# Redrawn side-work tables in a one-layer diffusion step: where weight splits, loads and dot products are emitted, and 69 transferred low parts for 64

## The chip, the cores and the metric

The kernel runs on one core of one Trainium2 chip. The metric is the device time of one execution in microseconds (us); before the change its median is 1312.32 us (three runs, 1312.31 to 1314.57). Lower is better.

## The reference

One inference step of a transformer layer (width 2048, hidden 8192) on two groups of 128 tokens, a prompt ("context") and a sample ("latent"), with the same weights for both:

```python
sh1, sc1, g1, sh2, sc2, g2 = split(silu(c) @ w_ada + b_ada, 6)
h = rms_norm(x) * norm1_w * (1 + sc1) + sh1
qa, ka, va, qb, kb, vb, ga, gb = split(h @ w_in)          # 2048 x 8704
oa = windowed_gqa(rms(qa), rms(ka), va, ...)              # rotary, sink logit, cached context keys
ob = neighbourhood_attention(rms(qb), rms(kb), vb, ...)   # 2-D bias, cached context keys
x = x + g1 * ((sigmoid(ga) * (oa @ w_br_a) + sigmoid(gb) * (ob @ w_br_b)) @ w_out)
h2 = rms_norm(x) * norm2_w * (1 + sc2) + sh2
x = x + g2 * (relu(h2 @ w_up) ** 2 @ w_down)
```

Everything is float32, and the outputs are x of both groups and the prompt's new keys and values.

## The kernel before

**Products in three parts.** TensorE multiplies in a reduced float32 form. Each operand is therefore split into a high part and a low part (the rest), and a product is three: high x high, high x low, low x high. A weight tile is 128 x 1024 (512 KB in `raw`, two row blocks of 512 columns). Its high part `wH` is a rounding copy on ScalarE (`copy`, line 103). Its low part `wL` is made in one of two ways. In the first, VectorE subtracts (`prep_b`, line 265). In the second (`minus_plus`, lines 271 and 272), ScalarE writes the negated high part, and a transfer issued by GpSimd reads the same weights from memory once more and adds them on top. The table `LO_DMA` lists the steps that use the second way, 64 of them.

**Steps.** The program has 456 weight steps in a fixed order, each with one tile and normally 12 matmuls: steps 0 to 71 the first columns of w_in, 72 to 135 the gates, 136 to 167 the branch products, 168 to 199 w_out (the last unit goes through its tiles twice, once for each group), 200 to 215 the first two blocks of w_up, then seven times a pair of up blocks (16 steps, from 216 + 32p) and a down unit (16 steps), and the last down unit from 440. The up pairs use a seven-product scheme over sums of weight blocks: an x step (even) and a y step (odd) together give the tiles `XH`, `XL`, `YB`, `tH`, `tL`, `uH`, `uL`, whose sums are made on VectorE (`y_sums`, `y_split`).

**Order.** Nothing is scheduled by a tool: each engine runs its instructions in the order in which the program emits them, and waits where an operand or a buffer isn't ready. All tiles come from one pool of 54 buffers, so a load waits until a buffer's last reader has finished. The loop `run` goes through the steps. At step i it emits

1. the loads (on SyncE's queue, SP) that stand up to `RUN[i]` steps further on than their place, which is four steps ahead of the step that uses the tile,
2. the transferred low parts of all steps up to i + `LOOK[i]` + 2,
3. the high parts up to i + `LOOK[i]` + `HIA[i]` and the low parts up to i + `LOOK[i]`,
4. the matmuls of step i,
5. the side work that the other tables place at step i.

```python
to = st["i"] + int(LOOK[st["i"]]) + 1
while by_dma and by_dma[0] < to + LO_AHEAD:
    prep_to(by_dma[0] - LO_AHEAD)
    ...
    lo_dma(wsteps[by_dma.pop(0)])
prep_to(to, int(HIA[st["i"]]))
st["mm"](st)
```

**Side work and its tables.** Part of the modulation is made as dot products on VectorE (`dot`, line 1522), two instructions for each entry of `DOTS1`, `DOTS` and `DOTS2`, with a load of 512 KB (`aT`) two steps ahead. The other part goes through TensorE in pairs (`ADA_AT`). `XS_AT` places the scaling of x by its norm. `POST` and `JOBS` place the head norms and the stages of the eight attention jobs. `STAT_AT` places the sums of activations for the up pairs. `M_AT`, `P_UP`, `T_UP` and `U_AT` place the way of an activation block to TensorE's layout: square, two copies into 16-bit planes (`pl`), a transposing transfer on SP (the flip, line 953), a copy that joins the planes (`fTa`), the high part (`a14H` for block 14) and the low part. In `U_AT` the nine numbers of a block are, in this order: relu, square, first plane copy, second plane copy, flip, first join, second join, high part, low part; they count from the first step of the down unit that follows the pair. A down unit that continues a sum starts with a copy of it into the accumulator on ScalarE (`seed`, the rows `acc<-dsum`).

Of the kernel before, what the change touches and what calls it, by code (L numbers as in the profile page):

```python
# [32 lines left out]
FB_DVE = 0  # L33
FB1 = 14
H_AT = 41
DOTS1 = [33, 33, 34, 34, 37, 37, 38, 40]
CHUNKS = [2, 2, 2, 4, 6]
NFAST = 8
FAST = {1: (0, 1, 2, 3, 4, 5, 6, 7), 2: (0, 1, 2, 3, 4, 5, 6, 7), 3: (0, 1, 2, 3, 4, 5, 6, 7), 4: (0, 1, 2, 3, 4, 5, 6, 7), 5: (0, 1, 2, 3, 4, 5, 6, 7), 6: (0, 1, 2, 3, 4, 5, 6, 7), 7: (0, 1, 2, 3, 4, 5, 6, 7)}
# [2 lines left out]
GATE_BACK = 6  # L42
SEED_IN = {3: -1, 4: 0}
SEED_N = (1, 2, 3)
HIA = "743311210111132014324131040001201410000110000000000002332001000011112200212113220010615154541000000011111000021124242135340100000000000031000100414311111003102301703025456797534544530325756887798374954110152262222132244304001211210111020001260102113330004210012121111315222074354363333101001172221556711321013044002233031111121033136010430110000042100334314355141111111100213210101100355521327503258336647833123224414211344122452723573333221344624430000011"
JOIN_LO = 0
SEED_AT = 3
LATE = [1, 0, 0]
ROW_AT = [5, 7, 9, 5]
DIRECT = (3,)  # L50
LO_DMA = [64, 69, 72, 76, 87, 94, 100, 105, 110, 118, 127, 130, 133, 140, 147, 154, 161, 168, 183, 194, 198, 200, 203, 210, 216, 218, 222, 224, 226, 228, 230, 234, 244, 252, 256, 258, 262, 269, 278, 286, 290, 294, 302, 311, 318, 324, 331, 341, 344, 352, 354, 358, 372, 375, 382, 388, 390, 408, 414, 416, 431, 440, 448, 449]
LO_AHEAD = 2

LOOK = "100010111213011164332413300140432203041131331184978600221153115896444435023551503161000543026403132431730112254700160210305438274262151200044577885121102695523366300410132115557812663450155370787570110000735967810745434464433361435371013573632034355244866131031202123201114423542406313307740004014332100388338122762544214363040032331021455957564224713121320243345442298736555517835112330012221110101284023045855132241353731143033251004422430024017145740026"
RUN = "221025555544432133333141100000012151100201121111335457745771402336611111032228530138889867423326226732531445635474877893335887476653143842350364750147441278656355112212111411132451349967889852473322462112246975487815248698865578999999996798443355158999999999987113346242776767998566866777744620011111001121698877377958546288750377448911084554544625666757246225681136864256726310000012522883734579997877872106899999999888999867820057664458624531421113413677"
CONST_AT = [50, 61, 73, 56, 91, 58]
ADA_AT = [None, 5, 11, 23, 23, 41, 28]
XS_AT = {1: 9, 2: 21, 3: 17}
POST = {('kvA', 0): [56, 68, 80], ('qA', 0): [61, 72, 77], ('qA', 1): [72, 73, 79], ('kB', 0): [79, 80, 83], ('qB', 0): [69, 83, 86], ('kB', 1): [92, 95, 101], ('qB', 1): [89, 95, 98]}
JOBS = [[84, 86, 87, 97, 101], [84, 84, 89, 92, 106], [84, 87, 89, 104, 114], [89, 95, 104, 107, 109], [103, 104, 107, 122, 125], [103, 105, 106, 111, 125], [106, 109, 116, 124, 125], [108, 111, 113, 118, 126]]  # L60
SS_AT = [74, 74, 128, 139]
T_AT = [3, 4]
PREP_IN = [5, 7]
DOTS = [45, 56, 56, 56, 56, 56, 56, 56, 57, 57, 60, 62, 63, 64, 65, 68, 72, 72, 72, 75, 78, 79, 79, 82, 83, 84, 84, 86, 88, 90, 90, 92, 93, 94, 96, 98, 98, 98, 99, 103, 105, 105, 107, 107, 109, 109, 111, 113, 113, 113, 114, 117, 121, 121, 122, 122, 123, 123, 126, 127, 131, 131, 132, 133, 133, 134, 134, 138, 139, 140, 141, 142, 144, 145, 146, 152, 153, 157, 158, 159, 160, 162, 166, 169, 174, 175, 178, 178, 179, 180, 183, 186, 187, 189, 190, 190]
DOTS2 = [233, 237, 239, 262, 271, 272, 297, 299, 331, 333, 333, 364, 365, 368, 395, 397, 425, 425, 427, 431, 433, 433, 433, 433, 437, 441, 441, 444, 444, 444, 444, 444]
STAT_AT = [-1, 0, 3, 8]
U_AT = [[[4, 4, 5, 7, 7, 10, 10, 10, 13], [5, 5, 7, 8, 11, 17, 18, 29, 29]], [[1, 1, 4, 4, 4, 5, 10, 26, 26], [10, 11, 11, 13, 13, 19, 27, 27, 27]], [[0, 0, 10, 10, 11, 16, 26, 26, 26], [11, 11, 13, 19, 20, 32, 32, 33, 33]], [[1, 1, 2, 4, 5, 9, 9, 11, 13], [2, 7, 7, 7, 7, 9, 12, 28, 28]], [[7, 9, 9, 9, 13, 19, 25, 25, 30], [2, 2, 2, 2, 5, 10, 12, 12, 16]], [[1, 2, 4, 4, 5, 9, 9, 11, 11], [2, 4, 4, 4, 6, 11, 11, 16, 18]], [[4, 7, 7, 7, 8, 10, 10, 14, 14], [2, 9, 9, 9, 10, 12, 13, 13, 14]]]
XLO_IN = True
STAY = [(3, 1), (3, 2), (5, 2), (5, 3)]
TL_DMA = [2, 3]  # L70
M_TE = (3,)
M_AT = [3, 10, 10]
FLIP = 2
P_UP = [2, 6]
T_UP = [6, 16]
COL = {"qA": 0, "kvA": 1024, "qB": 1536, "kB": 2560, "vB": 3584, "gA": 4608, "gB": 6656}


# [1 line left out]
def tile_hybrid_step(ctx: ExitStack, tc: tile.TileContext, a):  # L80
# [131 lines left out]
    def at(i, fn):  # L212
        cal.setdefault(i, []).append(fn)
# [5 lines left out]
    def load_at(i, fn):  # L219

        loads.append((i, len(loads), fn))
# [68 lines left out]

    by_dma = sorted(LO_DMA)

    def run():
        loads.sort(key=lambda x: x[:2])
        for st in wsteps:
            while loads and loads[0][0] <= st["i"] + int(RUN[st["i"]]):
                loads.pop(0)[2]()
            for j in sorted(j for j in pre if j <= st["i"]):
                for fn in pre.pop(j):
                    fn()  # L300
            to = st["i"] + int(LOOK[st["i"]]) + 1
            while by_dma and by_dma[0] < to + LO_AHEAD:
# [156 lines left out]
    def mod_pair(f):  # L459

        box, k0 = {}, 2 * f
        i = ADA_AT[f]
        for j in range(2):
# [7 lines left out]
    for f in range(1, FB1 // 2):  # L471
        mod_pair(f)
    for g, i in XS_AT.items():
        at(i, lambda g=g: x_scale(g))
# [208 lines left out]
    s0 = len([st for st in wsteps if st["key"] in first_units])  # L683
    load_at(CONST_AT[0], load_consts)
    at(CONST_AT[1], make_consts)
    load_at(CONST_AT[2], load_caches)
    load_at(CONST_AT[3], load_bias)
    for r in range(2):
        at(CONST_AT[4 + r], lambda r=r: mask_bias(r))

# [83 lines left out]

    for u, ps in POST.items():
        nh = 2 if u[0] == "kvA" else 4
# [120 lines left out]
    att_end = 0  # L897
    for (mix, s, g), js in zip([("A", 0, 0), ("A", 1, 0), ("A", 0, 1), ("A", 1, 1), ("B", 0, 0), ("B", 1, 0), ("B", 0, 1), ("B", 1, 1)], JOBS):
        need = [POST["kvA", 0][-1] + 1, POST["qA", g][-1] + 1] if mix == "A" else [
            POST["kB", g][-1] + 1, POST["qB", g][-1] + 1, end_of(("vB", g)) + 1]  # L900
        assert js[0] >= max(need) and list(js) == sorted(js)
# [105 lines left out]
    def br_unit(n):  # L1007
# [195 lines left out]
    def up_unit(n):  # L1203
# [514 lines left out]
```

## Time and profile before

| | |
|---|---|
| median of three runs | 1312.32 us (1312.31 to 1314.57) |
| the profiled execution's own time | 1325.06 us |
| its span, first to last instruction | 1323.3 us |
| mean granted TensorE clock | 0.995 |
| moved by DMA | 430.04 MB |
| transfers of accumulating low parts | 64 of weights, 2 of activations |

In the page's rows a group of instructions reads: line, engine, operation, output tile <- input tiles, shape, count, then busy us, mean ns of one, idle us of the engine just before them and what ended that idle time. In the rows of waits stand the waiting engine, tile and line, what ended the wait, and then total us, times and the longest. In the rows of windows each engine has its busy us; PEclk is the share of TensorE's clock that was granted.

### The profile page before, as it was taken

The numbers are of one execution on the slowest core, as the hardware profiler recorded it, in microseconds if no ns is written. First come the engines' busy times: TensorE is split into PE (matmuls) and PEld (weight loads), VectorE is DVE, ScalarE is ACT, GpSimd is POOL, SyncE is SP. The second block draws the span as 40 slices with busy tenths as digits, with TensorE's granted clock in tenths as the row PEclk, the third lists the DMA queues.
The fourth block names the chain that finished last, engine by engine and source line by source line (L and its number), as shares of the span: only waits on it lengthen the run. The fifth ranks groups of instructions, "written<-read, shape, count | busy, mean of one in ns | idle before, by whom it ended". The sixth has DMA issues, their size and how long they took to land.

```text
span 1323.3 us, 18149 instructions
## 1 busy us (share of the span) xinstructions
PE 1292.9 (98%) x6141; PEld 1047.6 (79%) x6142; DVE 1199.6 (91%) x1584; ACT 963.1 (73%) x1364; POOL 108.1 (8%) x128
## 2 busy tenths in 40 slices
PE   8999999999999999999999999999997999999988
PEld 4787788788888888787878888878886888788876
DVE  4495999999999999999899898999996999999987
ACT  5635668779776665737789897987896878897761
POOL 0000003213000000001101010100000000010110
PEclk9999999999999999999999999999998999999999
DMA  9999999999989999999799999988998999979995
GB/s 373 408 409 401 391 364 328 385 335 326 322 315 376 377 369 338 318 377 311 234 273 279 321 309 342 316 295 294 298 362 152 319 299 276 375 213 377 353 306 184
DMA packets 158285, 430.04 MB, mean 325 GB/s; under 512 B 53056, under 2 KB 54320, under 8 KB 158192
## 3 DMA queue, kind: packets, MB, share of 16 engines
q1 hardware_dynamic: 145264, 383.39, 79.3%
q0 software_dynamic: 12736, 45.39, 16.8%
q8 instruction: 48, 0.79, 0.2%
q14 instruction: 45, 0.37, 0.1%
q10 hardware_dynamic: 192, 0.10, 0.0%
HBM read 402.82 MB, written 14.99 MB: 316 GB/s over the span
## 4 chain that ended last, share of the span: by engine, by line
PE 63%; DMA 11%; issue 11%; DVE 9%; ACT 4%; POOL 1%; DVEq 0%; ACTq 0%; POOLq 0%; SPq 0%
PE acc L324 11%; PE acc L325 11%; PE acc L323 11%; PE acc L434 4%; PE acc L436 4%; PE acc L435 4%; PE Q L1296 4%; PE Q L1295 4%; PE Q L1297 4%; DMA raw<-in_w_down 3%; DMA raw<-in_w_upF 2%; DMA araw<-in_w_pair 1%; PE ps_ada L340 1%; DMA raw<-in_w_in 1%; DVE wL L265 1%
## 5 line engine op out<-in xcount | busy, mean ns | idle before, releaser
L103 ACT ACTIVATE wH<-raw 128x1024 fp32r<-128x1024 f32 (+1 forms) x347 | 347.2, 1043 | 94.6 <-DMA raw<-in_w_down 26.5
L265 DVE TENSOR_TENSOR wL<-raw,wH 128x1024 fp32r<-128x1024 f32 x303 | 356.3, 1222 | 25.0 <-ACT wH L103 14.7
L434 PE MATMUL acc<-wH,hH 128*128 128x512 f32 x276 | 108.5, 393 | 0.0
L436 PE MATMUL acc<-wH,hL 128*128 128x512 f32 x276 | 107.5, 389 | 0.0
L435 PE MATMUL acc<-wL,hH 128*128 128x512 f32 x276 | 107.5, 389 | 0.0
L323 PE MATMUL acc<-wH,hH 128*128 128x512 f32 x256 | 102.8, 402 | 0.0
L324 PE MATMUL acc<-wL,hH 128*128 128x512 f32 x256 | 100.0, 391 | 1.2 <-DVE wL L265 1.2
L325 PE MATMUL acc<-wH,hL 128*128 128x512 f32 x256 | 99.9, 390 | 0.0
L1522 DVE CUSTOM_DVE_ANT_0 junk<-aT,cB,cols 128x1024 uint8<-128x1024 f32 x68 | 87.6, 1288 | 0.8
L1522 DVE CUSTOM_DVE_ANT_0 aT<-aT,cB,cols 128x1024 f32<-128x1024 f32 x68 | 86.2, 1290 | 0.6
L1361 DVE TENSOR_TENSOR t<-raw 128x1024 f32<-128x1024 f32 x56 | 68.2, 1217 | 2.7 <-DMA raw<-in_w_upF 2.3
L1373 DVE TENSOR_TENSOR tL<-t,tH 128x1024 fp32r<-128x1024 f32 x56 | 68.2, 1217 | 2.6 <-ACT tH L103 2.5
L103 ACT ACTIVATE uH<-raw 128x1024 fp32r<-128x1024 f32 x56 | 58.9, 1051 | 13.9 <-DVE raw L1367 10.5
L1373 DVE TENSOR_TENSOR uL<-raw,uH 128x1024 fp32r<-128x1024 f32 x56 | 68.2, 1217 | 0.1
L103 ACT ACTIVATE XH<-raw 128x1024 fp32r<-128x1024 f32 x56 | 58.8, 1050 | 11.2 <-PE Q L1297 4.7
L434 PEld LDWEIGHTS acc<-wH,hH 128*128 128x128 f32 x276 | 51.8, 188 | 12.7 <-issue 2.1
L103 ACT ACTIVATE tH<-t 128x1024 fp32r<-128x1024 f32 x56 | 58.7, 1049 | 2.4 <-DVE t L1361 1.5
L436 PEld LDWEIGHTS acc<-wH,hL 128*128 128x128 f32 x276 | 51.8, 188 | 10.9
L435 PEld LDWEIGHTS acc<-wL,hH 128*128 128x128 f32 x276 | 51.8, 188 | 10.5
L324 PEld LDWEIGHTS acc<-wL,hH 128*128 128x128 f32 x256 | 48.2, 188 | 11.9 <-DVE wL L265 2.1
L325 PEld LDWEIGHTS acc<-wH,hL 128*128 128x128 f32 x256 | 48.1, 188 | 10.2
L323 PEld LDWEIGHTS acc<-wH,hH 128*128 128x128 f32 x256 | 48.1, 188 | 10.0 <-issue 0.5
(668 smaller groups left out, 3465.8 us busy)
## 6 DMA issues: line engine op xcount, KB each, us to landing
raw<-in_w_in SPq DMA_DIRECT2D x133, 512.0 KB, 10.1
raw<-in_w_down SPq DMA_DIRECT2D x128, 512.0 KB, 10.1
raw<-in_w_upF SPq DMA_DIRECT2D x112, 512.0 KB, 6.6
aT<-in_w_adaT SPq DMA_DIRECT2D x72, 512.0 KB, 10.2
aT<-in_w_gT SPq DMA_DIRECT2D x64, 512.0 KB, 10.2
araw<-in_w_pair SPq DMA_DIRECT2D x56, 512.0 KB, 10.1
raw<-in_w_out SPq DMA_DIRECT2D x32, 512.0 KB, 9.6
XL<-in_w_upF POOLq DMA_DIRECT2D x26, 512.0 KB, 8.6
```

The costliest lines, as they stand in the source:

```text
L103: act.activation(out, in_, AF.Copy)
L265: dve.tensor_tensor(st["lo"], st["raw"], st["hi"].bitcast(F32), op=OP.subtract)
L323: pe.matmul(acc[tb], sh, wh[:, k, :], start=f, stop=False, **kw)
L324: pe.matmul(acc[tb], sh, wl[:, k, :], start=False, stop=False, **kw)
L325: pe.matmul(acc[tb], sl, wh[:, k, :], start=False, stop=l, **kw)
L434: pe.matmul(acc[tb], sh, wh[:, k, :], start=kt == 0 and k == 0 and not held and not seeded, stop=False, **kw)
L435: pe.matmul(acc[tb], sh, wl[:, k, :], start=False, stop=False, **kw)
L436: pe.matmul(acc[tb], sl, wh[:, k, :], start=False, stop=last and k == 1 and not hold, **kw)
L1295: pe.matmul(acc, stat[0], hi, start=f, stop=False)
L1361: dve.tensor_tensor(t.rearrange("p (a n) -> p a n", a=2), X.rearrange("p (a n) -> p a n", a=2), Y[:, 0:512].unsqueeze(1).to_broadcast([P, ...
L1373: dve.tensor_tensor(b[n + "L"], v, b[n + "H"].bitcast(F32), op=OP.subtract)
L1522: dve.tensor_tensor_reduce(out, box["raw"], cB[s, tag], 1.0, dst if second else baT[:, part, fb:fb + 1], OP.mult, OP.add, dst)
```

## The change

No function changes, only the tables. Five more steps make their low part by transfer (69), of which 37 are at steps that were not in the list and 32 of the old ones leave it. The tables of loads, look-ahead, dot products, attention jobs, flips and joins all have new values; the number of their entries stays the same. `CONST_AT`, `POST`, `JOBS`, `XS_AT` and the like, not shown, move by some steps in both directions.

```diff
-DOTS1 = [33, 33, 34, 34, 37, 37, 38, 40]
+DOTS1 = [32, 32, 32, 32, 33, 35, 39, 40]
...
-HIA = "743311210111132014324131040001201410000110000000000002332001000011112200212113220010615154541000000011111000021124242135340100000000000031000100414311111003102301703025456797534544530325756887798374954110152262222132244304001211210111020001260102113330004210012121111315222074354363333101001172221556711321013044002233031111121033136010430110000042100334314355141111111100213210101100355521327503258336647833123224414211344122452723573333221344624430000011"
+HIA = "001100001000411222332210054210000242143001000003224543223212012110001000011000245401621101454713440001010010120224222132503400000000013000000000000000010131110211232212338877341224100003402572200201156510010314003222565435425221131010100001070110024131341212000000072722311155142252214431223432124469900111213200011000110121233321000101202101112113334211562210553325232131400121111004000010000000102103626513410000004521221100001322111000002114432895666510"
...
-LO_DMA = [64, 69, 72, 76, 87, 94, 100, 105, 110, 118, 127, 130, 133, 140, 147, 154, 161, 168, 183, 194, 198, 200, 203, 210, 216, 218, 222, 224, 226, 228, 230, 234, 244, 252, 256, 258, 262, 269, 278, 286, 290, 294, 302, 311, 318, 324, 331, 341, 344, 352, 354, 358, 372, 375, 382, 388, 390, 408, 414, 416, 431, 440, 448, 449]
+LO_DMA = [58, 68, 77, 84, 88, 94, 95, 99, 105, 109, 112, 116, 119, 123, 128, 129, 136, 139, 147, 154, 159, 168, 179, 190, 194, 200, 201, 203, 216, 218, 220, 222, 224, 226, 228, 230, 235, 247, 260, 262, 264, 279, 286, 288, 290, 294, 305, 311, 320, 324, 331, 341, 352, 354, 356, 360, 365, 378, 382, 384, 388, 390, 414, 416, 431, 436, 447, 449, 450]
...
-LOOK = "100010111213011164332413300140432203041131331184978600221153115896444435023551503161000543026403132431730112254700160210305438274262151200044577885121102695523366300410132115557812663450155370787570110000735967810745434464433361435371013573632034355244866131031202123201114423542406313307740004014332100388338122762544214363040032331021455957564224713121320243345442298736555517835112330012221110101284023045855132241353731143033251004422430024017145740026"
-RUN = "221025555544432133333141100000012151100201121111335457745771402336611111032228530138889867423326226732531445635474877893335887476653143842350364750147441278656355112212111411132451349967889852473322462112246975487815248698865578999999996798443355158999999999987113346242776767998566866777744620011111001121698877377958546288750377448911084554544625666757246225681136864256726310000012522883734579997877872106899999999888999867820057664458624531421113413677"
...
+LOOK = "042431211022233002010456720126530002442122131444566203233273666985468546244512333161330650346525041211755332033612371521115535201040103365267886563685525772869672131236353222145537254664237378468624325692748837854460100040025676721266676754538440441535778752001112000012016212520524222888985222110220323487888642695697575160520110540363778977011202365562300130020441268427554569010101233034205572624177384155747542741364422354054574858226434305244795322733"
+RUN = "323520002452847511233115361322757443213699552341124866643641212024512326576868461000338955244328413764623367636789889881417522311278788972533554334565450317796251432020000211073450333310002113003787889988857876776180567899998786778888999999897346616379999987997666899899996568798368768999998767879995413303889871498999999999998498788875482311721003768836666702575449999898814586439745458986834777776778888529998777888899998889857113464711476163001122228988"
-ADA_AT = [None, 5, 11, 23, 23, 41, 28]
+ADA_AT = [None, 5, 13, 20, 22, 40, 32]
-XS_AT = {1: 9, 2: 21, 3: 17}
+XS_AT = {1: 11, 2: 11, 3: 8}
...
-STAT_AT = [-1, 0, 3, 8]
-U_AT = [[[4, 4, 5, 7, 7, 10, 10, 10, 13], [5, 5, 7, 8, 11, 17, 18, 29, 29]], [[1, 1, 4, 4, 4, 5, 10, 26, 26], [10, 11, 11, 13, 13, 19, 27, 27, 27]], [[0, 0, 10, 10, 11, 16, 26, 26, 26], [11, 11, 13, 19, 20, 32, 32, 33, 33]], [[1, 1, 2, 4, 5, 9, 9, 11, 13], [2, 7, 7, 7, 7, 9, 12, 28, 28]], [[7, 9, 9, 9, 13, 19, 25, 25, 30], [2, 2, 2, 2, 5, 10, 12, 12, 16]], [[1, 2, 4, 4, 5, 9, 9, 11, 11], [2, 4, 4, 4, 6, 11, 11, 16, 18]], [[4, 7, 7, 7, 8, 10, 10, 14, 14], [2, 9, 9, 9, 10, 12, 13, 13, 14]]]
+STAT_AT = [6, 2, -1, 8]
+U_AT = [[[6, 6, 6, 9, 10, 11, 14, 17, 17], [10, 10, 10, 10, 16, 19, 23, 23, 28]], [[0, 4, 4, 8, 12, 15, 26, 26, 30], [1, 8, 10, 12, 12, 18, 19, 27, 31]], [[3, 7, 9, 9, 10, 21, 26, 28, 29], [6, 13, 19, 19, 21, 27, 28, 31, 32]], [[3, 4, 5, 5, 7, 11, 11, 11, 14], [3, 8, 9, 9, 9, 10, 19, 31, 33]], [[4, 4, 8, 9, 11, 19, 21, 29, 29], [3, 4, 4, 5, 6, 11, 11, 11, 11]], [[0, 2, 4, 5, 5, 8, 8, 14, 14], [1, 9, 9, 10, 10, 24, 25, 28, 28]], [[4, 8, 9, 9, 9, 10, 10, 10, 12], [3, 4, 9, 9, 9, 14, 14, 14, 15]]]
...
-M_AT = [3, 10, 10]
+M_AT = [1, 9, 9]
...
-P_UP = [2, 6]
-T_UP = [6, 16]
+P_UP = [2, 9]
+T_UP = [7, 16]
```

More of the change, by code (lines that the diff above doesn't have):

```diff
@@ L56 @@
-CONST_AT = [50, 61, 73, 56, 91, 58]
-ADA_AT = [None, 5, 11, 23, 23, 41, 28]
-XS_AT = {1: 9, 2: 21, 3: 17}
-POST = {('kvA', 0): [56, 68, 80], ('qA', 0): [61, 72, 77], ('qA', 1): [72, 73, 79], ('kB', 0): [79, 80, 83], ('qB', 0): [69, 83, 86], ('kB', 1): [92, 95, 101], ('qB', 1): [89, 95, 98]}
-JOBS = [[84, 86, 87, 97, 101], [84, 84, 89, 92, 106], [84, 87, 89, 104, 114], [89, 95, 104, 107, 109], [103, 104, 107, 122, 125], [103, 105, 106, 111, 125], [106, 109, 116, 124, 125], [108, 111, 113, 118, 126]]
+LOOK = "042431211022233002010456720126530002442122131444566203233273666985468546244512333161330650346525041211755332033612371521115535201040103365267886563685525772869672131236353222145537254664237378468624325692748837854460100040025676721266676754538440441535778752001112000012016212520524222888985222110220323487888642695697575160520110540363778977011202365562300130020441268427554569010101233034205572624177384155747542741364422354054574858226434305244795322733"
@@ new lines @@
+RUN = "323520002452847511233115361322757443213699552341124866643641212024512326576868461000338955244328413764623367636789889881417522311278788972533554334565450317796251432020000211073450333310002113003787889988857876776180567899998786778888999999897346616379999987997666899899996568798368768999998767879995413303889871498999999999998498788875482311721003768836666702575449999898814586439745458986834777776778888529998777888899998889857113464711476163001122228988"
+CONST_AT = [51, 62, 76, 61, 86, 70]
@@ L61 @@
+ADA_AT = [None, 5, 13, 20, 22, 40, 32]
+XS_AT = {1: 11, 2: 11, 3: 8}
+POST = {('kvA', 0): [60, 71, 76], ('qA', 0): [62, 63, 72], ('qA', 1): [66, 70, 76], ('kB', 0): [73, 74, 87], ('qB', 0): [65, 74, 85], ('kB', 1): [96, 99, 100], ('qB', 1): [87, 100, 104]}
+JOBS = [[81, 82, 89, 99, 102], [78, 82, 89, 96, 110], [82, 83, 91, 107, 110], [87, 99, 103, 106, 109], [99, 104, 107, 113, 125], [102, 102, 106, 114, 127], [109, 109, 116, 119, 121], [107, 111, 112, 116, 125]]
 SS_AT = [74, 74, 128, 139]
@@ L63 @@
 PREP_IN = [5, 7]
-DOTS = [45, 56, 56, 56, 56, 56, 56, 56, 57, 57, 60, 62, 63, 64, 65, 68, 72, 72, 72, 75, 78, 79, 79, 82, 83, 84, 84, 86, 88, 90, 90, 92, 93, 94, 96, 98, 98, 98, 99, 103, 105, 105, 107, 107, 109, 109, 111, 113, 113, 113, 114, 117, 121, 121, 122, 122, 123, 123, 126, 127, 131, 131, 132, 133, 133, 134, 134, 138, 139, 140, 141, 142, 144, 145, 146, 152, 153, 157, 158, 159, 160, 162, 166, 169, 174, 175, 178, 178, 179, 180, 183, 186, 187, 189, 190, 190]
-DOTS2 = [233, 237, 239, 262, 271, 272, 297, 299, 331, 333, 333, 364, 365, 368, 395, 397, 425, 425, 427, 431, 433, 433, 433, 433, 437, 441, 441, 444, 444, 444, 444, 444]
-STAT_AT = [-1, 0, 3, 8]
-U_AT = [[[4, 4, 5, 7, 7, 10, 10, 10, 13], [5, 5, 7, 8, 11, 17, 18, 29, 29]], [[1, 1, 4, 4, 4, 5, 10, 26, 26], [10, 11, 11, 13, 13, 19, 27, 27, 27]], [[0, 0, 10, 10, 11, 16, 26, 26, 26], [11, 11, 13, 19, 20, 32, 32, 33, 33]], [[1, 1, 2, 4, 5, 9, 9, 11, 13], [2, 7, 7, 7, 7, 9, 12, 28, 28]], [[7, 9, 9, 9, 13, 19, 25, 25, 30], [2, 2, 2, 2, 5, 10, 12, 12, 16]], [[1, 2, 4, 4, 5, 9, 9, 11, 11], [2, 4, 4, 4, 6, 11, 11, 16, 18]], [[4, 7, 7, 7, 8, 10, 10, 14, 14], [2, 9, 9, 9, 10, 12, 13, 13, 14]]]
+DOTS = [44, 44, 47, 48, 52, 55, 56, 56, 59, 61, 61, 61, 67, 67, 67, 67, 67, 73, 73, 76, 76, 77, 80, 83, 84, 84, 84, 85, 89, 90, 90, 91, 91, 92, 92, 94, 100, 100, 100, 105, 107, 107, 107, 107, 107, 108, 110, 111, 113, 113, 114, 120, 120, 120, 121, 123, 123, 125, 125, 125, 129, 129, 131, 132, 134, 134, 136, 137, 137, 137, 143, 143, 144, 146, 149, 149, 150, 152, 157, 158, 159, 167, 167, 172, 172, 174, 176, 180, 180, 181, 181, 183, 187, 187, 189, 190]
+DOTS2 = [235, 238, 239, 268, 271, 273, 298, 302, 332, 334, 337, 362, 362, 363, 397, 397, 423, 425, 425, 432, 432, 432, 433, 433, 437, 441, 441, 441, 442, 444, 444, 444]
+STAT_AT = [6, 2, -1, 8]
+U_AT = [[[6, 6, 6, 9, 10, 11, 14, 17, 17], [10, 10, 10, 10, 16, 19, 23, 23, 28]], [[0, 4, 4, 8, 12, 15, 26, 26, 30], [1, 8, 10, 12, 12, 18, 19, 27, 31]], [[3, 7, 9, 9, 10, 21, 26, 28, 29], [6, 13, 19, 19, 21, 27, 28, 31, 32]], [[3, 4, 5, 5, 7, 11, 11, 11, 14], [3, 8, 9, 9, 9, 10, 19, 31, 33]], [[4, 4, 8, 9, 11, 19, 21, 29, 29], [3, 4, 4, 5, 6, 11, 11, 11, 11]], [[0, 2, 4, 5, 5, 8, 8, 14, 14], [1, 9, 9, 10, 10, 24, 25, 28, 28]], [[4, 8, 9, 9, 9, 10, 10, 10, 12], [3, 4, 9, 9, 9, 14, 14, 14, 15]]]
 XLO_IN = True
```

## The prediction

> **What bounds the kernel now.** I read the page first, then who TensorE waited for, then windows around the waits, then single instructions in them.
>
> ```profile
> span 1323.3 us, 18149 instructions
> PE 1292.9 (98%) x6141; PEld 1047.6 (79%) x6142; DVE 1199.6 (91%) x1584; ACT 963.1 (73%) x1364; POOL 108.1 (8%) x128
> ...
> DMA  9999999999989999999799999988998999979995
> ...
> q1 hardware_dynamic: 145264, 383.39, 79.3%
> q0 software_dynamic: 12736, 45.39, 16.8%
> ```
>
> TensorE is busy in 98% of the span: its instructions are the floor, and the change adds and takes none of them. What side work can win is the 30.4 us in which PE is idle (1323.3 - 1292.9) and what a cold clock costs after it. VectorE has 91%, ScalarE 73%, the DMA engines 96% (79.3 + 16.8). The waits of PE, with what ended them (total, times, longest):
>
> ```profile
> PE acc L323 <- ACT acc L103: 5.9, 1, 5.9
> PE acc L323 <- ACT a14H L103: 3.3, 1, 3.3
> PE acc L324 <- DVE wL L265: 2.8, 4, 1.4
> PE acc L1118 <- DVE wL L265: 1.7, 1, 1.7
> ...
> PE Q L1295 <- ACT dsum L103: 1.2, 1, 1.2
> ...
> PE Q L1296 <- DVE tL L1373: 0.8, 1, 0.8
> PE ps_T L930 <- DVE g_gA L1017: 0.7, 1, 0.7
> PE ps_gr L1535 <- DVE gc_g L1522: 0.7, 1, 0.7
> PE acc L325 <- DVE a14L L976: 0.5, 1, 0.5
> ...
> PE Q L1296 <- DMA XL<-in_w_upF: 0.5, 1, 0.5
> ```
>
> Two single waits stand apart from many small ones. In the windows that hold them the clock fell too (PE busy, PEld, DVE, ACT, POOL, PEclk, DMA share, GB/s):
>
> ```profile
> 1000.00:1050.00 50.00, 42.88 (x180) 34.44 (x179) 41.92 (x46) 36.29 (x43) 3.17 (x4) 0.93 0.84 246
> ...
> 1250.00:1300.00 50.00, 46.13 (x196) 37.28 (x195) 45.09 (x62) 32.17 (x39) 5.44 (x8) 0.97 0.95 311
> ```
>
> The first cost 5.9 + 1.2 of wait and 50 x (1 - 0.93) = 3.5 us of clock: 10.6 us. The second cost 3.3 + 0.5 and 50 x (1 - 0.97) = 1.5: 5.3 us. Together 15.9. The profiled execution took 1325.06 us, 1.8 over its span and 12.7 over the median of 1312.32; without these two it would stand at 1309.2. So of the 15.9 us only about 3.1 can be in a timed run, and the small waits (DVE's 2.8 + 1.7 + 0.8 + 0.7 + 0.7 = 6.7) are what the median still has to give. I make the sum against the profile and against the median side by side.
>
> **Part 1: five splits leave VectorE, and the others are put earlier.** A low part made on VectorE is one subtraction (L265). Made by transfer it is a negated copy on ScalarE (L271), an issue on GpSimd (L272) and a second reading of the 512 KB. The rows, busy and mean ns:
>
> ```profile
> L265 DVE TENSOR_TENSOR wL<-raw,wH 128x1024 fp32r<-128x1024 f32 x303 | 356.3, 1222 | 25.0 <-ACT wH L103 14.7
> ...
> L1522 DVE CUSTOM_DVE_ANT_0 junk<-aT,cB,cols 128x1024 uint8<-128x1024 f32 x68 | 87.6, 1288 | 0.8
> ```
>
> ```profile
> L271 ACT ACTIVATE wL<-wH 128x1024 fp32r<-128x1024 f32 x38 | 40.2, 1059 | 1.1 <-PE acc L324 0.2
> ...
> L272 POOL DMA_DIRECT2D XL<-in_w_upF x26 | 22.7, 872 | 221.7 <-ACT XL L271 136.5 <-DVE t L1361 30.4 <-DVE tL L1373 22.1
> ```
>
> VectorE: -5 x 1.222 = -6.1 us. ScalarE: +5 x 1.059 = +5.3 us, covered by its idle 27%; if that cover failed in one place, a copy that PE needs would be 1 us later there. GpSimd: +5 x 0.872 = +4.4 us, covered by its 8%.
>
> Whether 6.1 us of VectorE matter is decided by its queue where PE waits. Step 170 shows it: the split stands behind two dot products, and the DVE runs without a gap.
>
> ```profile
> 140.40 3.49 DVE L265 TENSOR_TENSOR wL<-raw,wH 128x1024 fp32r<-128x1024 f32 x3
> ...
> 549.35 1.28 DVE L1522 CUSTOM_DVE_ANT_0 aT<-aT,cB,shT 128x1024 f32<-128x1024 f32 x1
> ...
> 550.56 3.49 DVE L265 TENSOR_TENSOR wL<-raw,wH 128x1024 fp32r<-128x1024 f32 x3
> ```
>
> ```profile
> 142.02 0.39 PE L434 MATMUL acc<-wH,hH 128*128 128x512 f32 x1
> ...
> 259.15 0.50 PE L324 MATMUL acc<-wL,hH 128*128 128x512 f32 x1 [0.92 <-DVE wL L265]
> ...
> 551.83 0.50 PE L324 MATMUL acc<-wL,m1H 128*128 128x512 f32 x1 [1.39 <-DVE wL L265]
> ```
>
> Following run() with both tables (a split is emitted at the first step i with i + LOOK[i] at or above its own): step 170's is emitted at 169 before (LOOK 3 there) behind 149 splits and 182 dot instructions, and at 167 after (LOOK 6) behind 145 and 178. That is 4 x 1.222 + 4 x 1.288 = 10.0 us less ahead of it, against a wait of 1.39. The same count for the others: step 199 (the 1.7) 175 and 208 become 171 and 207, 6.2 us less; step 101 has 91 and 89, then 90 and 88, 2.5 us less; step 298 has four splits fewer, 4.9 us; step 77 (the 0.92 at 259.15) is itself made by transfer. So all five waits, 2.8 + 1.7 = 4.5 us, should go. Bounds: nothing, if each wait only moves to another split, and -6.7, if all five DVE rows go. I take -4.5, because every one of the five has more taken from ahead of it than it waited. What is late next is the transfers (part 2).
>
> The other VectorE and ScalarE tables (dot products, jobs, x_scale, ADA_AT, STAT_AT) move work between steps and cost no instruction more. They have no price of their own here beyond the queue counts above; one place goes the other way: step 36's split stands behind ten dot instructions of DOTS1 instead of six, 4 x 1.288 = 5.2 us more. It ends at 141.6 (140.40 and a third of 3.49) for a step that PE reaches at 142.02, so the bounds are 0 and +4.8. I take 0, because the loads for these dots are emitted at step 25 instead of 31, so that they need not stand at the same time.
>
> **Part 2: where the transfers now stand.** Of the 69, 14 lie in the gate steps (11 before), and all eight x steps of the first fast pair (216 to 230) have one instead of seven. The nearest row that shows a late one is there: issued at 692.62, it let PE wait at step 224.
>
> ```profile
> 692.62 0.87 POOL L272 DMA_DIRECT2D XL<-in_w_upF  x1 [11.31 <-ACT XL L271]
> ```
>
> ```profile
> 688.69 0.39 PE L1295 MATMUL Q<-XH,h20H 128*128 128x512 f32 x1
> ...
> 703.83 0.50 PE L1296 MATMUL Q<-XL,h22H 128*128 128x512 f32 x1 [0.47 <-DMA XL<-in_w_upF]
> ```
>
> This one took 703.83 - 692.62 = 11.2 us. It was emitted at step 218, which PE began at 688.69, and was of use 15.1 us later. After the change step 224's is emitted at 220 and step 228's at 224, four steps or about 10 us ahead each. Read as time, both would be late by 15.1 - 10 = 5 us: +10. But emission is an order and no time, and ScalarE had 24.77 us of work in these 25:
>
> ```profile
> 687.00:712.00 25.00, 24.53 (x109) 19.94 (x108) 24.71 (x31) 24.77 (x30) 3.46 (x4) 1.00 1.03 243
> 455.00:542.00 87.00, 86.38 (x382) 71.49 (x383) 83.78 (x116) 50.56 (x51) 3.46 (x4) 1.00 1.05 349
> ```
>
> Ahead of these two negations only 1.1 and 1.7 us of its work are added. So the bounds are +1.1 and +10; I take +1.5, as the order is the nearer row. Steps 105 and 112 (three steps ahead, 11 to 12 us) are alike: 0 to +7, taken +0.5.
>
> The five more transfers also load the DMA engines: q0 takes 16.8% x 1323.3 = 222 us for 45.39 MB, so 4.9 us per MB and 2.57 us for 0.524 MB; five make 12.8 us. Bounds 0 (hidden) and +12.8 (every us paid). I take 0: at shares of 1.03 and 1.05 the engines moved 243 GB/s in the one window above and 349 in the other, so the share counts packets that wait as well as bytes, and the loads' queue waits more for buffers than for transfers:
>
> ```profile
> SPq L231 <- PE acc L325: 150.5, 53, 9.3
> ...
> SPq L231 <- DMA raw<-in_w_down: 33.3, 31, 3.2
> ```
>
> The Trainium skill (DMA: Bandwidth & Descriptors, "Issuing engines are not separate DMA queues") speaks against the change here: transfers of all issuers run on the same 16 engines and interleave. By that rule the engines could be the bound, and the sum would be 12.8 us higher; it is weighed as the last rival.
>
> **Part 3: loads earlier, high parts less far ahead.** RUN rises from 4.54 to 5.31 steps in the mean, LOOK from 3.03 to 3.66, HIA falls from 2.10 to 1.76. ScalarE's splits wait for landings:
>
> ```profile
> ACT wH L103 <- DMA raw<-in_w_down: 26.5, 17, 8.5
> ```
>
> More RUN and less HIA mean that ScalarE meets a landed tile more often. The 5.9 us wait is of this kind (a seed copy queued behind a late load). In a timed run I count nothing for it, as little of it recurs there; in the profile 10.6 us. The cost is buffers: the SP row of 150.5 us above says that a load asked for earlier may only wait longer, with SP's flips behind it. Bounds -1.6 and +3; taken 0.
>
> **Part 4: the last pair of relu halves.** a14 was joined at 1258.6 (1255.98 and 2.57), but its copy a14H stood behind the join of a15, which waited for its flip:
>
> ```profile
> 1255.98 2.57 ACT L103 ACTIVATE fTa<-pTa 128x1024 uint16<-128x1024 uint16 x2
> ...
> 1263.46 1.39 ACT L103 ACTIVATE fTa<-pTa 128x1024 uint16<-128x1024 uint16 x1 [4.00 <-DMA pTa<-pla]
> ...
> 1270.94 1.04 ACT L103 ACTIVATE a14H<-fTa 128x1024 fp32r<-128x1024 f32 x1
> ```
>
> U_AT moves that copy from step 438 to 434, ahead of the join of a15. It takes the 5.3 us of this wait away. Against it, both flips are now issued at 433 (432 and 434 before), and a14's join follows one step behind: give back up to 2. Profile: -3.3. Timed: at most 3.1 us of the two disturbances is there, so half of it, -1.5 (bounds -5.3 and +2). M_AT, P_UP and T_UP shift flips and joins by one to three steps and are part of the same bounds.
>
> **The sum.** Median: 1312.3 - 4.5 - 1.5 + 1.5 + 0.5 = 1308.3. Profile: 1325.1 - 4.5 - 10.6 - 3.3 + 2.0 = 1308.7, or 1319 if a late landing like the first recurs.
>
> **Rivals.** (1) The transfers come too late (slower). Steps 224 and 228 pay the 10 us above; with -4.5 and -1.5 that is 1316.3. It decides once the two are more than 4 us late each. For it: 224's has no slack now. Against it: only 1.1 to 1.7 us are put ahead of them. (2) Nothing measurable: for each wait that goes another comes, since PE is busy 98% already and any of 456 steps can be the next late one; 1312. For it: five of the waits here are under 1.4 us, so what frees one step by a few us can cost another as much. (3) More goes than I count: all of DVE's 6.7, the 3.1, the 1.2 and 0.5, with no new wait: 1300.8. (4) The DMA engines are the bound: 12.8 - 6.0 gives 1319.1. For it: share 96%, over 1.00 in the two windows of part 2; against it their GB/s.
>
> **How the numbers follow.** A measurement of this kernel tells 0.2% (2.6 us) from nothing: faster is below 1309.7, slower above 1314.9. Forecast 0.38 (own range 1305 to 1310), rival 3 0.13, rival 2 0.23, rival 1 0.20, rival 4 0.06. A forecast that comes out 1.5 us high falls into "same", one as much low stays faster: I leave 0.50 faster, 0.24 same, 0.26 slower. The range runs from rival 3 to rival 4, 1301 to 1319, and leaves about 0.1 outside.
>
> **What would show it.** Right: L265 x298, L271 x71 in all; no PE wait for wL at L324 or L1118 above 1 us; no wait for a14H; PEclk 1.00 in all windows from 50 us to the end. Wrong: PE waits on XL of 5 us near 703 to 720; the small waits add up to 6 us or more again under other names; the raw loads' time to landing rises by more than 1 us.

## The result, and the profile after

The kernel after takes 1307.81 us (median of 21 runs, 1306.48 to 1314.63) against 1315.05 us for the kernel before beside it (21 runs, 1311.74 to 1321.00): a ratio of 0.9950, with a 95% interval of 0.9936 to 0.9963, so 4.9 to 8.4 us faster. The median of before was 1312.32 in the three runs shown earlier, is 1315.05 here, and lay between 1315.24 and 1317.5 in the sessions of the experiments. Ratios below are therefore always to the runs of before in the same session.

The page of the kernel after, the lines that answer to those of before:

```profile
span 1308.8 us, 18194 instructions
...
PE 1291.1 (99%) x6142; PEld 1045.4 (80%) x6142; DVE 1196.0 (91%) x1579; ACT 964.8 (74%) x1369; POOL 108.9 (8%) x133
...
q1 hardware_dynamic: 145264, 383.39, 79.1%
q0 software_dynamic: 13456, 48.01, 17.6%
...
L265 DVE TENSOR_TENSOR wL<-raw,wH 128x1024 fp32r<-128x1024 f32 x298 | 351.7, 1224 | 26.4 <-ACT wH L103 18.3
```

The profiled execution took 1310.53 us. VectorE has five splits fewer, ScalarE and GpSimd five instructions more, and the accumulating queue moved 2.62 MB more. PE's idle time fell from 30.4 to 17.7 us (1308.8 - 1291.1). The waits of PE in it:

```profile
PE acc L324 <- DVE wL L265: 2.1, 4, 0.8
PE ps_h L1153 <- DVE h2f L1145: 1.5, 1, 1.5
...
PE acc L323 <- ACT wH L103: 1.2, 1, 1.2
...
PE Q L1295 <- ACT up L1187: 0.7, 2, 0.6
PE acc L1228 <- ACT acc L103: 0.7, 1, 0.7
```

The 5.9 us for `acc` and the 3.3 us for `a14H` are gone, and none above 1.5 us has come. The two windows that held them, columns as before:

```profile
1000.00:1050.00 50.00, 50.00 (x222) 41.40 (x221) 48.65 (x55) 43.51 (x50) 3.98 (x5) 1.00 0.89 272
1250.00:1300.00 50.00, 49.28 (x217) 39.77 (x216) 46.99 (x64) 29.05 (x35) 5.91 (x9) 1.00 0.88 292
```

PEclk is 1.00 in both. At the end of the last pair ScalarE now does this:

```profile
1250.44 2.58 ACT L103 ACTIVATE fTa<-pTa 128x1024 uint16<-128x1024 uint16 x2 [3.32 <-PE acc L324]
1253.05 1.06 ACT L103 ACTIVATE a14H<-fTa 128x1024 fp32r<-128x1024 f32 x1
...
1256.02 2.59 ACT L103 ACTIVATE fTa<-pTa 128x1024 uint16<-128x1024 uint16 x2
```

The copy `a14H` stands right behind its own joins and ahead of a15's, and it is done 4.5 us before PE reads it at 1258.6.

### The profile page after: what moved, and what is told of

The parts are those of the page before. It is cut to its first block, busy times and chain, and to the rows that moved or that the text cites. A ratio compares the mean times of both kernels' runs of the same rounds, so it can differ in the third digit from the quotient of the medians.

```text
span 1308.8 us, 18194 instructions
## 1 busy us (share of the span) xinstructions
PE 1291.1 (99%) x6142; PEld 1045.4 (80%) x6142; DVE 1196.0 (91%) x1579; ACT 964.8 (74%) x1369; POOL 108.9 (8%) x133
## 4 chain that ended last, share of the span: by engine, by line
PE 69%; DVE 2%; DMA 2%; ACT 2%; issue 1%; POOL 0%; DVEq 0%; ACTq 0%
PE acc L324 15%; PE acc L325 15%; PE acc L323 15%; PE Q L1296 7%; PE Q L1295 7%; PE Q L1297 7%; DMA pTm<-plm 1%; DMA raw<-in_w_down 1%; DVE wL L265 1%; ACT wH L103 1%; PE ps_PT L858 0%; PE ps_o L882 0%; PE ps_S L811 0%; PE ps_o L886 0%; DVE aT L1522 0%
## 5 line engine op out<-in xcount | busy, mean ns | idle before, releaser
L265 DVE TENSOR_TENSOR wL<-raw,wH 128x1024 fp32r<-128x1024 f32 x298 | 351.7, 1224 | 26.4 <-ACT wH L103 18.3
L103 ACT ACTIVATE uH<-raw 128x1024 fp32r<-128x1024 f32 x56 | 58.8, 1051 | 14.4 <-DVE raw L1367 10.2
L325 PEld LDWEIGHTS acc<-wH,hL 128*128 128x128 f32 x256 | 48.1, 188 | 10.1
## 6 DMA issues: line engine op xcount, KB each, us to landing
raw<-in_w_down SPq DMA_DIRECT2D x128, 512.0 KB, 10.2
aT<-in_w_gT SPq DMA_DIRECT2D x64, 512.0 KB, 10.3
araw<-in_w_pair SPq DMA_DIRECT2D x56, 512.0 KB, 10.2
```

The costliest lines, as they stand in the source:

```text
L103: act.activation(out, in_, AF.Copy)
L265: dve.tensor_tensor(st["lo"], st["raw"], st["hi"].bitcast(F32), op=OP.subtract)
L325: pe.matmul(acc[tb], sl, wh[:, k, :], start=False, stop=l, **kw)
```

## The experiments

The table gives every kernel's median and its ratio to the kernel before of its own session.

| label | edit | median, us | ratio to before, 95% |
|---|---|---|---|
| a_oldlo | after, old LO_DMA | 1348.23 | 1.0222, 1.0191 to 1.0253 |
| b_newlo | before, new LO_DMA | 1354.57 | 1.0285, 1.0253 to 1.0317 |
| a_oldrun | after, old RUN, LOOK, HIA | 1424.39 | 1.0823, 1.0784 to 1.0862 |
| a_olduat | after, old U_AT, STAT_AT, M_AT, P_UP, T_UP | 1364.37 | 1.0351, 1.0313 to 1.0390 |
| bef2 | before, second profile | 1312.44 | (one run) |
| a_u6old | after, old last row of U_AT | 1314.43 | 0.9992, 0.9971 to 1.0012 |
| a_no224 | after, two transfers fewer | 1309.77 | 0.9958, 0.9939 to 0.9977 |
| b_u6new | before, new last row of U_AT | 1310.56 | 0.9965, 0.9944 to 0.9986 |
| b_a14h | before, one number of U_AT | 1312.91 | 0.9955, 0.9937 to 0.9974 |
| aft2 | after, second profile | 1311.55 | 0.9948, 0.9925 to 0.9970 |
| a_more4 | after, four transfers more | 1318.83 | 1.0017, 0.9998 to 1.0035 |
| a_less10 | after, ten transfers fewer | 1317.10 | 1.0003, 0.9985 to 1.0020 |

**Whole tables exchanged.** The first idea was to take the change apart table by table.

```diff
 a_oldlo:  -LO_DMA of after      +LO_DMA of before
 b_newlo:  -LO_DMA of before     +LO_DMA of after
 a_oldrun: -RUN, LOOK, HIA of after   +those of before
 a_olduat: -U_AT, STAT_AT, M_AT, P_UP, T_UP of after   +those of before
```

> The changed kernel with the old list of 64 transferred low parts; everything else stays new. Theory 1 (VectorE's queue: the splits taken from it are what made the waits for wL go): about 1312, since 25 of the 31 splits that leave VectorE before step 199 are partly put back and step 77 is one of them; waits for wL at L324 and L1118 of 4 us or more in all. Rival (run-ahead: the loads and splits emitted earlier did it, the transfers nothing): 1308 as the changed kernel, waits for wL as there (2.1 us). Rival (transfers cost DMA time): 1305 or less, raw loads landing sooner by 0.3 us or more.

> The kernel before with the new list of 69 transferred low parts alone. Theory 1 (VectorE's queue): 4.5 us under the kernel before, near 1310.5, with no wait for wL at step 77 and shorter ones at steps 101, 170 and 199. Rival (run-ahead): as before, 1315, or slower, since the transfers stand at steps that the old look-ahead was not made for. Rival (transfers cost DMA time): 1318 or more.

> The changed kernel with the old RUN, LOOK and HIA; everything else stays new. Theory 1 (VectorE's queue, mostly by the transfers): 1310, two us of waits for wL back where LOOK set the order. Rival (run-ahead did it): 1315, as before or worse, with ScalarE waiting more than 26 us for raw of w_down, and single long waits of PE of 3 us or more with the clock below 1.00 in their window.

> The changed kernel with the old U_AT, STAT_AT, M_AT, P_UP and T_UP (flips, joins and the high and low parts of activations); everything else stays new. If part 4 of the prediction holds, the wait for a14H near the end is back: 3 to 4 us of wait and 1.5 us of clock in the profile, 1 to 5 us in the time, so 1309 to 1313. Rival (that wait came from the old loads and run-ahead, not from where the copy stood): no wait for a14H, 1308.

The theory missed in all four: each kernel loses 2% to 8%, far more than the whole change moves. Of the rivals, only those came true that said "slower" without a size: "or slower" and "1318 or more" in b_newlo, and "worse", with single long waits, in a_oldrun (whose third sign, ScalarE's wait for `raw` of w_down above 26 us, is 23.3 there). No rival had a loss of this size. The waits of PE in a_oldrun, the worst:

```profile
PE acc L324 <- DVE wL L265: 24.7, 11, 5.1
PE Q L1296 <- DMA XL<-in_w_upF: 18.4, 4, 15.0
PE acc L323 <- ACT acc L103: 7.1, 1, 7.1
PE acc L323 <- ACT up L103: 6.5, 2, 4.4
PE ps_o L882 <- DVE oLA L891: 6.0, 1, 6.0
```

The new list of transfers loses 2.85% in the old tables, and the old list loses 2.2% against before in the new ones. So a table's worth can't be read from exchanging it whole: in these four, tables of one set lose among those of the other. (The new RUN, LOOK and HIA in the kernel before were not tried.) One line could be read from these kernels all the same. A wait for `a14H` stood in b_newlo (10.0 us) and a_olduat (4.2 us), which have the old U_AT, and was absent from a_oldlo and a_oldrun, which have the new one. The next kernels therefore change single entries.

**The kernel before once more.**

> The kernel before, unchanged, profiled once more, to size the term of the sum that came out too small: how much of the two disturbances of the first profile (15.9 us) is in an ordinary execution. Theory A (they belong to the schedule: steps 340 and 440 of the old tables are late in most executions, and the three runs of 1312.3 were lucky): the wait for a14H at step 440 returns with 2 us or more, a seed wait at step 340 with some us, and the run takes 1315 to 1325. Theory B (chance of that one execution, as the prediction took it): neither wait is above 1 us, PEclk is 1.00 in the windows 1000 to 1050 and 1250 to 1300, the run takes 1311 to 1313. Rival C: they come, but at other places.

1312.44 us, and a mixture of A and B: the time is B's, the clock at step 440 is A's, and the wait there (1.05 us) lies between the two. The windows of this second profile:

```profile
1000.00:1050.00 50.00, 49.74 (x220) 40.86 (x219) 49.76 (x55) 41.13 (x47) 3.16 (x4) 1.00 0.85 290
...
1260.00:1270.00 10.00, 9.47 (x35) 7.56 (x35) 9.96 (x13) 5.37 (x7) 0.00 (x0) 0.83 1.03 408
```

The first disturbance (10.6 us at 1002) is not there. The second is, at step 440, even in this execution, 12.6 us shorter than the first profiled one. PE there:

```profile
1259.40 0.50 PE L323 MATMUL acc<-wH,a14H 128*128 128x512 f32 x1 [1.05 <-ACT a14H L103]
...
1260.66 0.50 PE L325 MATMUL acc<-wH,a14L 128*128 128x512 f32 x1 [0.53 <-DVE a14L L976]
...
1261.84 0.63 PE L323 MATMUL acc<-wH,a14H 128*128 128x512 f32 x1
...
1264.40 0.63 PE L323 MATMUL acc<-wH,a14H 128*128 128x512 f32 x1
1264.83 0.43 PE L324 MATMUL acc<-wL,a14H 128*128 128x512 f32 x1
```

1.05 + 0.53 us of wait, and then matmuls of 0.63 instead of 0.39 us for 3.4 us. 10 x (1 - 0.83) is 1.7 us more, half of the 3.4, so the clock was halved there and step 440 costs 3.3 us here (in the first profile of before 5.3). On ScalarE the copy again stands behind a15's join and what follows it:

```profile
1250.80 1.37 ACT L103 ACTIVATE fTa<-pTa 128x1024 uint16<-128x1024 uint16 x1 [2.37 <-DMA pTa<-pla]
...
1258.31 1.04 ACT L103 ACTIVATE a14H<-fTa 128x1024 fp32r<-128x1024 f32 x1
```

The waits for `wL`:

```profile
PE acc L324 <- DVE wL L265: 1.2, 2, 0.9
...
PE acc L1118 <- DVE wL L265: 0.9, 1, 0.9
```

2.1 us with nothing changed, where the first profile had 4.5. They are three of the same five: steps 77, 101 and 199 wait again (0.9, 0.3 and 0.9 us); the 1.39 us at step 170 and the 0.17 us at step 298 did not come back. PE's idle time in this profile is 18.2 us (1310.7 - 1292.5), hardly more than the 17.7 of the kernel after: most of the fall from 30.4 was the first profile's own.

**The last row of U_AT, from both sides.** The row of blocks 14 and 15 in the last pair:

```diff
 a_u6old (after):
-[[4, 8, 9, 9, 9, 10, 10, 10, 12], [3, 4, 9, 9, 9, 14, 14, 14, 15]]
+[[4, 7, 7, 7, 8, 10, 10, 14, 14], [2, 9, 9, 9, 10, 12, 13, 13, 14]]
 b_u6new (before): the reverse
```

> The kernel after with only the last row of U_AT (blocks 14 and 15 of the last pair) put back: a14's joins and high part at steps 435, 435 and 439 again, flips two steps apart. Theory (part 4 of the prediction): the wait of PE for a14H at step 440 comes back with 3 to 5 us and some clock after it, and the median rises by 2 to 6 us over the kernel after. Rival 1 (another copy is late instead of it, whatever the row): no a14H wait and a change within 1 us. Rival 2 (one row too is fitted to the rest, as the whole tables were): new waits at other places before step 430 too, and a loss of 10 us or more.

> The kernel before with only the last row of U_AT from the new tables (blocks 14 and 15). Theory (part 4): no wait for a14H at step 440 in its profile, and the median falls by 1.5 to 5 us under the kernel before. Rival 1 (the wait goes to the next copy, a15H or the low part, or to step 440's weights): within 1 us of before. Rival 2 (the row fits only the new tables): new waits between steps 424 and 456 and a slower kernel by 3 us or more.

Both as the theory has it. (By the row's numbers, counted from step 424, a14's joins and its copy stand at 434, 434 and 438 in the old row; a_u6old's expectation has them one step later.) With the old row the kernel after has lost its gain (0.9992): 5.5 us by the two ratios, and 4.7 us against a_no224 of the same session, which has the new row. With the new row alone the kernel before is 4.7 us faster (0.9965). The waits of a_u6old begin with the one that was expected, and 1250 to 1300 has the cold clock again:

```profile
PE acc L323 <- ACT a14H L103: 4.0, 1, 4.0
PE acc L324 <- DVE wL L265: 1.9, 4, 0.7
PE ps_h L1153 <- DVE h2f L1145: 1.5, 1, 1.5
```

```profile
1250.00:1300.00 50.00, 45.50 (x195) 36.70 (x194) 44.50 (x60) 26.40 (x34) 5.91 (x9) 0.97 0.87 279
```

**One number of that row.**

```diff
 b_a14h (before):
-[[4, 7, 7, 7, 8, 10, 10, 14, 14], ...
+[[4, 7, 7, 7, 8, 10, 10, 10, 14], ...
```

> The kernel before with one number of U_AT changed: the high part of block 14 in the last pair at 10 instead of 14, so that the copy a14H is emitted at step 434, right behind its joins, and the flips and joins of both blocks stay where they were. It tells the place of the copy from the place of the flips. Theory (part 4: the copy stands behind a15's join, which waits for its flip): no wait for a14H at step 440, PEclk 1.00 in the window 1250 to 1300, the median 3 to 6 us under the kernel before, as the whole row had it (1310.56 against 1315.24). Rival 1 (the flips had to move as well): a14H still 1 to 4 us late, less than 2 us gained. Rival 2 (the copy now waits in front of other work of ScalarE): a new wait between steps 434 and 440 of 2 us or more and no gain.

The theory holds: 4.6 us under its kernel before by the medians, no wait for `a14H`, PEclk 1.00 at 1250 to 1300. ScalarE in b_a14h:

```profile
1248.81 2.59 ACT L103 ACTIVATE fTa<-pTa 128x1024 uint16<-128x1024 uint16 x2
1251.43 1.06 ACT L103 ACTIVATE a14H<-fTa 128x1024 fp32r<-128x1024 f32 x1
...
1255.46 1.38 ACT L103 ACTIVATE fTa<-pTa 128x1024 uint16<-128x1024 uint16 x1 [2.02 <-DMA pTa<-pla]
```

a15's join still waits 2.02 us for its flip, which did not move; the copy just no longer stands behind it. So the place of the copy alone does it.

**The kernel after beside it.**

> The kernel after, unchanged, beside the others on one chip and with a second profile. Theory: 1307 to 1309 us, no wait for a14H, and under 1 us for every wait in which the two profiles of after differ. It tells how much is left to all other tables together: if nearly all of the gain is the one row of U_AT, this stands within 2 us of the kernel before with that row alone (b_a14h here, 1310.56 for the whole row). Rival: it stands 3 us or more under them, and the other tables carry half of the gain.

The theory holds on the comparison: 1311.55 us, 1.4 us under b_a14h, with ranges that overlap widely (1307.22 to 1314.21 and 1308.44 to 1317.42). The median is 2.5 us higher than expected, in a session in which before too was higher (1317.5). By the ratios the two lie 0.9 us apart, with intervals that overlap almost wholly: what all other tables together are worth beyond the one number, these runs can't tell from nothing. One sign missed: the first profile of after has a wait of 1.2 us for `wH` that this one has not.

**Two transfers taken back.**

```diff
 a_no224 (after), LO_DMA:
-... 222, 224, 226, 228, 230, ...
+... 222, 226, 230, ...
```

> The kernel after with the low parts of steps 224 and 228 made on VectorE again (67 transfers). Rival 1 of the prediction held these two to be late. Theory (they came in time and the trace shows no XL wait there): taking them out gains nothing; VectorE gets 2.4 us more in its fullest stretch, and the median rises by 0 to 4 us. Rival (each transfer costs its 2.57 us of DMA engine time): two fewer save up to 5 us. Rival (fitted schedule): the two splits on VectorE make new waits in the steps 224 to 240 of 5 us or more.

1309.77 us at 0.9958, not told apart from after: no gain from taking them out. `XL` of step 224 in the kernel after:

```profile
694.43 0.86 POOL L272 DMA_DIRECT2D XL<-in_w_upF  x1 [11.47 <-ACT XL L271]
...
704.88 0.39 PE L1296 MATMUL Q<-XL,h22H 128*128 128x512 f32 x1
```

It landed 6.0 us after the issue, 4.4 us before PE needed it, with no wait: it was not late.

**More and fewer transfers.**

```diff
 a_more4 (after):  LO_DMA + 81, 89, 158, 330
 a_less10 (after): LO_DMA - 77, 159, 235, 260, 279, 305, 331, 360, 378, 436
```

> The kernel after with four more low parts by transfer, at the four steps where PE still waits for wL (81, 89, 158, 330): 73 in all. VectorE has 4.9 us less, the DMA engines 10.3 us more. Theory (as the prediction has it, the engines are not the bound): within 0 to -2 us of the kernel after, and those four waits (2.1 us in all) gone. Rival 4 of the prediction (the DMA engines are the bound): 10 us slower. Rival (transfers three steps ahead are late): waits for DMA at these steps of 1 us or more.

> The kernel after with ten low parts put back on VectorE, spread over the span (steps 77, 159, 235, 260, 279, 305, 331, 360, 378, 436): 59 transfers. VectorE has 12.2 us more, ScalarE 10.6 us less, the DMA engines 25.7 us less. Theory (part 1: a split leaves VectorE, and its time matters only where PE waits for the queue): some of the ten places show a wait for wL, 3 to 8 us in all, the median 3 to 8 us over the kernel after. Rival A (VectorE at 91% is nearly the bound): 10 to 12 us slower or more. Rival B (the DMA engines are the bound): faster by 5 us or more. Rival C (VectorE's time is hidden): within 2 us.

a_more4 was meant to remove the last four waits for `wL`. It did (of the waits for `wL` one of 1.0 us is left, for a transferred one), but the theory missed: it is 7.3 us slower than aft2 in the same session, with no overlap of the runs (1316.37 to 1322.67). As a number that is near rival 4's 10 us, but the loads did not land later in general (`in_w_upF` 5.8 us, in aft2 6.0; `in_w_down` 10.2 in both). The loss has one main place, with 4.2 us of wait and 1.7 us of clock after it, of the 10.3 us between the two profiles' spans; the second row, early in the program, has nothing to do with it:

```profile
PE acc L323 <- DVE g_gA L1010: 4.2, 1, 4.2
PE ps_S L811 <- ACT T_kvA L103: 2.3, 1, 2.3
```

The chain to it starts at one flip on SP's queue. SP and GpSimd in a_more4:

```profile
496.43 11.86 SPq L953 DMA_TRANSPOSE pTm<-plm  x1
508.38 1.36 SPq L1061 DMA_DIRECT2D x<-in_x_prompt  x1
...
513.15 2.05 SPq L231 DMA_DIRECT2D raw<-in_w_br_b  x1
```

```profile
498.24 0.87 POOL L272 DMA_DIRECT2D wL<-in_w_br_b  x1 [3.89 <-ACT wL L271]
502.18 0.87 POOL L272 DMA_DIRECT2D wL<-in_w_br_b  x1 [3.07 <-ACT wL L271]
```

and the same flip in aft2, which has one transfer (at 498.02) beside it:

```profile
496.62 4.05 SPq L953 DMA_TRANSPOSE pTm<-plm  x1
500.77 0.51 SPq L1061 DMA_DIRECT2D x<-in_x_prompt  x1
...
505.20 0.38 SPq L231 DMA_DIRECT2D raw<-in_w_br_b  x1
```

With the added transfer, step 158's, the flip held SP 11.86 instead of 4.05 us. The next load behind it went out 7.6 us later (508.38 against 500.77), ScalarE waited 14.9 us for the flip (9.1 in aft2), VectorE stood behind ScalarE and then behind a late load, and PE waited 4.2 us:

```profile
516.74 2.58 ACT L103 ACTIVATE fTm<-pTm 128x1024 uint16<-128x1024 uint16 x2 [14.91 <-DMA pTm<-plm]
```

```profile
520.44 1.23 DVE L976 TENSOR_TENSOR m0L<-fTm,m0H 128x1024 fp32r<-128x1024 f32 x1 [5.43 <-ACT m0H L103]
523.28 1.23 DVE L265 TENSOR_TENSOR wL<-raw,wH 128x1024 fp32r<-128x1024 f32 x1 [1.62 <-DMA raw<-in_w_br_b]
```

The DMA engines moved little in that time, in a_more4 and then in aft2:

```profile
505.00:510.00 5.00, 5.00 (x24) 4.14 (x23) 4.96 (x10) 0.00 (x0) 0.00 (x0) 1.00 1.25 94
```

```profile
505.00:510.00 5.00, 5.00 (x23) 4.13 (x23) 4.93 (x9) 3.21 (x3) 0.00 (x0) 1.00 1.05 378
```

94 GB/s at a share of 1.25, against 378. The dip itself is in the kernel after too: in its first profile, with one transfer beside the flip, the engines moved 106 GB/s in the same window, ScalarE waited 12.9 us for the flip, and PE soon after 1.2 us for `wH` and 0.8 us for `wL`. But the flip landed 20.2 us after its issue in a_more4, and after 10.1 to 13.8 us in the four profiles that have the new tables here without the added transfer. So the loss is not 2.57 us of engine time for every transfer, but sits mostly at one place. That the added transfer made it by slowing the flip beside it is argued from the order of times and not shown: no run added this transfer alone, and in a_less10, with none beside it, the flip held SP 7.05 us.

a_less10 is 5.6 us slower than aft2 (1315.57 to 1318.65, no overlap), inside the theory's 3 to 8, but the waits are not where the theory put them: `wL` has 2.2 us in four waits, like aft2's 1.4, and the larger ones are for `XL` (2.4) and `tL` (2.3), at places that were not followed further. More or fewer transfers both lose, which excludes VectorE or the DMA engines as a plain bound in this range.

## Why the prediction came out near, point by point

**What bounds the kernel.** Right in its places, wrong in one step: "Together 15.9 ... only about 3.1 can be in a timed run". It was worked out from one profile and a median of three runs that lay low. The second disturbance is in ordinary executions: 5.3 us in the first profile, 3.3 in the second, a wait of 4.0 us in a_u6old, and 4.6 to 4.7 us of the median when it alone is removed. The first one (10.6 us) did not come back in bef2. Runs of before reach 1324.7 us and those of after 1314.6, so it may recur in some; that was not shown.

**Part 1** (taken -4.5) is the term that was too large: about 0. The five named waits are gone, as worked out. But in the unchanged kernel's second profile only 2.1 us of such waits stood, so 2.4 of the 4.5 us did not come back, and the kernel after has 2.1 us again, at steps 81, 89, 158 and 330. That is rival 2's mechanism: for each wait that goes another comes. That parts 1 to 3 together are worth about nothing is what a_u6old measures (below); part 1 by itself was not measured. The deduction that more is taken from ahead of each split than it waited was true of each place, not of the sum over all places.

**Part 2** (taken +1.5 and +0.5) cost nothing: no wait for `XL` in the kernel after, and a_no224 gained nothing. Choosing the order over the clock time was right. Taking 0 for the DMA engines was right for these five transfers: the landing of `in_w_upF` went from 6.6 to 5.7 us, that of `in_w_down` from 10.1 to 10.2. a_more4, which loses mostly at one place, suggests that it matters where they stand more than how many there are. The Trainium skill (DMA: Bandwidth & Descriptors, "Issuing engines are not separate DMA queues") says that transfers from all issuers share the same engines and interleave; the flip of 11.86 us beside two transfers is in keeping with that.

**Part 3** (taken 0) could not be measured by itself. Its tables are worth 8% in their own surroundings (a_oldrun) and, with all others but U_AT's last row, nothing that can be measured against the old set in its own: a_u6old stands at 0.9992 of before, with an interval of -0.3% to +0.1%.

**Part 4** (taken -1.5 in a timed run, -3.3 in the profile) is the term that was too small, and most of the gain: -4.7 by b_u6new, -4.6 by b_a14h, and -5.5 from a_u6old to after by their ratios. The mechanism is the one described, the copy behind a join that waits for its flip: in the profiles of before, bef2 and a_u6old, with the old row, that join waited 4.0, 2.4 and 4.7 us for its flip, and PE 3.3, 1.0 and 4.0 us for `a14H`. The "give back up to 2" for the flips was not seen: b_a14h leaves them alone, b_u6new moves them, and both gain as much. The profile's own figure was the better one. Discounting it to the part that one low median left room for threw away a wait that two profiles would have shown to be regular.

**The sum.** 1308.3 forecast, 1307.81 measured. But the gain is 6.6 us by the ratio of its session (4.9 to 8.4), not 4.0, and the terms are about 0, 0 and -5 in place of -4.5, +2.0 and -1.5. Three misjudged terms and a low base cancelled, so that the number came out this near is luck. The profile, forecast at 1308.7, took 1310.53. The signs named as right are there: L265 x298, L271 x71, no wait for `wL` above 1 us, none for `a14H`, PEclk 1.00 in every window of 50 us from 50 to 1300 (0.84 in the last 9 us, in which PE ends at 1304). None of the signs named as wrong is. Rivals 1 and 4 failed at their places, rival 3 in the small waits, which came back; rival 2 was right on the small waits and wrong on the total.

## What to carry to other kernels

In an in-order program, look for the copy that stands behind a wait it doesn't depend on; one number that moved `a14H` ahead of such a wait brought about as much as a complete new set of tables. Before a wait in a profile is counted as chance or as rule, profile the same kernel twice. Tables that were fitted together can't be priced by exchanging one: change single entries, from both sides.

## What the runs showed of the hardware

- Short waits can cool the clock, but their length alone does not decide it: in bef2 1.05 and 0.53 us of idle PE within 2.3 us were followed by 3.4 us of matmuls at half speed, and a wait of 2.2 us (for `g_gA` in b_a14h) had PEclk at 0.84 in its 10 us. A single wait of 1.5 us (for `h2f` in the kernel after) left PEclk at 1.00, and so did two of 1.2 and 0.8 us within 2.5 us (near 518 us in the same profile), more idle time than in bef2. The Trainium skill (TensorE: Matmul & The Clock Gate, "The HAM clock gate (the "warmup" mystery)") gives a free-running window of about 3.4 us and two speeds, the slow one after at least one idle window; the 3.4 us at half speed agrees, a whole idle window was not needed here, and why so little idle time sufficed, no run tells.
- Flips with accumulating transfers near them landed later. Of the 266 flips in the fourteen profiles, 173 had none issued within 6 us before or after their own issue and landed after 5.4 us in the median; 72 had one and took 8.1; 20 had two and took 10.5; the one with three is a_more4's of 20.2. Plain loads beside them differ too, so this is a relation and not a price.
